# Value projections of four heads in one pass: 512 moving columns into four PSUM banks, with the gate projections moved between them

## The chip, the core and the metric

The kernel runs on one core of a Trainium2 chip, in one launch. Five engines work side by side, each with its own instruction stream: TensorE (PE, with its weight loads listed as PEld), VectorE (DVE), ScalarE (ACT), GpSimd (POOL) and SyncE (SP), which here issues nearly all DMA transfers. An engine runs its instructions in the order in which they stand; it waits on semaphores that other engines and transfers raise. The metric is the device time of one execution in microseconds (us), lower is better. The kernel before took 1098.91 us, the median of three runs (1098.56 to 1100.02).

## The reference, cut to what matters

One layer on 512 tokens of width 2048: a norm, one big projection `z = u @ w_in` (2048 by 8192), eight heads of chunkwise retention and eight heads of differential attention, gates, an output projection, and a gated side input.

```python
u = rmsnorm(h, attn_norm)
z = u @ w_in                       # rq 512 | rk 512 | rv 1024 | rg 1024 | dq 1024 | dk 1024 | dv 1024 | dg 1024 columns
rq, rk = rope(rq), rope(rk) * RET_DK ** -0.5
ro = retention(rq, rk, rv)         # chunks of 64: scores * decay inside, state across
ro = rmsnorm(ro) * ret_gn * silu(rg)
dq, dk = rmsnorm(dq), rmsnorm(dk)
attn = softmax(q0 k0) - lam * softmax(q1 k1)      # block-causal, per head
do = rmsnorm(attn @ dv) * diff_subln * 0.2 * silu(dg)
h = h + concat(ro, do) @ w_out
gate = sigmoid(rmsnorm(h) @ w_ple_gate)
out = h + gate * (p @ w_ple_proj)
```

Everything is float32. The two parts of a head that the change touches are `rv` and `dv`, the values: 128 columns of `w_in` for each head.

## The kernel before

**Precision.** A float32 operand is split into a high and a low part (`split`, lines 103 to 110: ACT writes the high part, DVE the difference). A product is three matmuls (`mm3`, lines 112 to 115): high by high, high by low, low by high, summed in PSUM. Line 113, 114 and 115 are these three, for every projection.

**Projections.** Tokens are the moving side for all but the values: `proj_fm` (line 170) makes the columns stationary, 128 at a time, and moves all 512 tokens, so that one call gives two blocks of 128 columns in two PSUM banks. The values are wanted with tokens on partitions: `proj_v` (line 180) makes 128 tokens stationary and moves 256 weight columns, the values of two heads; four token blocks share two banks, two blocks to a bank (`v_products`, line 140). A call of either kind runs over 16 blocks of the contraction, two at a time, and its weights come in four transfers of 512 KB through `wraw` (two buffers) and are split into `whi` and `wlo` (four buffers each). At the end `done(acc)` empties the banks: for the values `split_v` (line 193), which scales by the column `rcol` of the row norm.

**PSUM.** There are eight banks: four with the tag `acc` for projections, taken in turn; two `sc`, one `tp`, one `o` for everything else. A projection that takes a bank waits until what read that bank last is through.

**Order.** The program is written by hand and then scheduled. `run(job)` advances a projection; each `yield` is a tick of `clock`, and each tick also issues the steps that are due in `agenda`. The steps are the small work: norms of q and k (`QK`), scores and softmax (`SCORES`), transposes (`TURNS`), attention times values (`VALUES`) and the head's norm (`NORMS`), all at fixed numbers of ticks after a pair's `dk` is finished. The last norm of a pair comes 32 ticks after it. A projection is eight ticks long.

**Stages.** (1) `dv` of heads 0 and 1 together with `dq` of the same pair, while x and the weights still arrive (lines 276 to 304), then `row_norm` (line 208), which gives `rcol` and the row factor `R1`. This `dv0` takes two of the four `acc` banks. (2) The loop over four pairs of attention heads (line 476): dq, dk, dv, dg. (3) `rq0`, `rk0` into the four `acc` banks and `rv0` into the two `sc` banks (lines 489 to 492), with the steps of the last pair between them; then `flush`. (4) Retention, whose SBUF pools `rp` and `rc` take the memory of the attention pool `dp`: cosine and sine tables `cr` and `sr` are loaded (lines 504, 505) and multiplied by `R1`, `rope` (line 509) turns q and k, and rv1, rq1, rk1, rv2, rv3 follow, with retention steps `queue_ret` (line 562) after each value projection. (5) Gates, `w_out`, `w_gate`, outputs.

**Where a bank of q is read.** In `rope`, line 514 copies quarters of the bank (ACT), line 515 multiplies the bank by `cr` (DVE); only then is it free. So `rq0`'s banks are held until `cr` has been loaded.

Of the kernel before, what the change touches and what calls it, by code (L numbers as in the profile page):

```python
# [38 lines left out]
def f(ap):  # L39
    return ap.bitcast(F32)  # L40
# [3 lines left out]
def tile_layer(  # L44
# [86 lines left out]

    def fm_products(acc, k, nk, wh, wl, mh, ml):
# [137 lines left out]
    with ExitStack() as st:  # L270
        xp = st.enter_context(tc.tile_pool(name="xp", bufs=1))
        ssum = xp.tile([P, S], F32, name="ssum")

        warm = bank("tp", 1, "warm")
        wide = xp.tile([P, S], F32R, name="wide")
        nc.vector.memset(f(wide), 1.0)
        for _ in range(WARM):
            nc.tensor.matmul(warm, lhsT=wide[:, :P], rhs=wide, start=True, stop=True)  # L280
        start = [[bank(*tag, f"acc_{name}0_{j}") for j in range(2)]
                 for tag, name in ((("acc", 4), "dv"), (("sc", 2), "dq"))]
        for k in range(KB):
            xt = xp.tile([P, S], F32, tag=f"xt{k}", name=f"xt{k}")
            nc.sync.dma_start(xt, xT[k * P:(k + 1) * P, :])
            if k % 2 == 0:
                raw, wh, wl = ([wpool.tile([P, 2, CW], dt, tag=tag, name=f"{tag}{i}_{k}", bufs=n)
                                for i in range(2)] for tag, dt, n in
                               (("wraw", F32, 2), ("whi", F32R, 4), ("wlo", F32R, 4)))
            for i, off in enumerate((OFF_DV, OFF_DQ)):  # L290
                nc.sync.dma_start(raw[i][:, k % 2, :], w_in[k * P:(k + 1) * P, off:off + CW])
# [5 lines left out]
            for i in range(2):  # L297
                split(wh[i][:, k % 2, :], wl[i][:, k % 2, :], raw[i][:, k % 2, :])
# [51 lines left out]
    with ExitStack() as st:  # L350
# [29 lines left out]
        def diff_steps(h, pair):  # L380
# [118 lines left out]
    with ExitStack() as st:  # L499
# [62 lines left out]
        def queue_ret(h, qkv):  # L562
            s, v, n = ret_steps(h, qkv)
# [5 lines left out]
        for g in range(2):  # L569
            qkv = {}  # L570

            def q_done(acc, g=g, qkv=qkv):
                for j in range(2):
                    t = rope(acc[j], f"q{g}_{j}")
                    for i, (half, oth) in enumerate(((A0, A1), (A1, A0))):
                        qd = rc.tile([P, S], F32R, tag=f"qd{j}{i}", name=f"qd{g}_{j}{i}")
                        nc.scalar.activation(qd[half], t[half], AF.Copy)
                        nc.vector.tensor_copy(qd[oth], f(qd)[half])

                        qz = rc.tile([P, S], F32R, tag=f"qz{j}{i}", name=f"qz{g}_{j}{i}")  # L580
                        nc.gpsimd.memset(f(qz)[oth], 0.0)
                        nc.vector.tensor_tensor(qz[half], t[half], f(qd)[half], ALU.subtract)
                        qkv["q", 4 * g + 2 * j + i] = qd, qz

            def k_done(acc, g=g, qkv=qkv):
                for j in range(2):
                    t = rope(acc[j], f"k{g}_{j}")
                    for i, (half, oth) in enumerate(((A0, A1), (A1, A0))):
                        ks = rc.tile([P, S], F32R, tag=f"ks{j}{i}", name=f"ks{g}_{j}{i}")
                        nc.scalar.activation(ks[half], t[half], AF.Copy)  # L590
                        nc.vector.tensor_tensor(ks[oth], t[half], f(ks)[half], ALU.subtract)
                        qkv["k", 4 * g + 2 * j + i] = ks

            if g == 0:
                q_done(ahead[0])
                k_done(ahead[1])
            else:
                run(proj_fm(w_in, OFF_RQ + g * CW, KB, u_hi, u_lo, f"rq{g}", q_done))
                run(proj_fm(w_in, OFF_RK + g * CW, KB, u_hi, u_lo, f"rk{g}", k_done))
            for hp in range(2 * g, 2 * g + 2):  # L600
                def v_done(acc, hp=hp, qkv=qkv):
                    mine = {**qkv, "v": split_v(acc, rp, f"rv{hp}")}
                    queue_ret(2 * hp, mine)
                    queue_ret(2 * hp + 1, mine)

                if hp == 0:
                    v_done(ahead[2])
                else:
                    run(proj_v(OFF_RV + hp * CW, f"rv{hp}", v_done))
# [175 lines left out]
```

## Time and profile before

| what | us |
|---|---|
| three runs | 1098.91, 1098.56, 1100.02 |
| the profiled execution | 1099.53 |
| its span in the trace | 1097.8 |
| PE busy | 1085.7 |
| DVE busy | 652.9 |
| ACT busy | 569.4 |

The span is what the trace covers; about 1.7 us of the profiled execution lie outside it. Matmuls overlap one another in the trace: one starts before the one ahead has ended. So the time that a matmul costs is read from the distance of two starts, not from its duration; a PE that is busy for 99% of the span only says that no gap is longer than such an overlap. An engine's idle time is shown in square brackets behind an instruction, with what ended it; DMA issue is shown as SPq.

Columns of the views below. Timeline: start and duration in us, engine, line, operation, output<-inputs with their shapes, and how many like it follow one another (x). Busy time by stretch: the stretch in us, its length, then busy us (and instructions) of PE, PEld, DVE, ACT and POOL, the granted clock as a share of full speed, the DMA engines' busy share, and GB/s. Waits: who waits <- for whom, total us, how often, the longest. Groups: as in the timeline, then busy us in total, mean ns of one, idle us before them.

### The profile page before, as it was taken

The numbers are of one execution on the slowest core, as the hardware profiler recorded it, in microseconds if no ns is written. First come the engines' busy times: TensorE is split into PE (matmuls) and PEld (weight loads), VectorE is DVE, ScalarE is ACT, GpSimd is POOL, SyncE is SP. The second block draws the span as 40 slices with busy tenths as digits, with TensorE's granted clock in tenths as the row PEclk, the third lists the DMA queues.
The fourth block names the chain that finished last, engine by engine and source line by source line (L and its number), as shares of the span: only waits on it lengthen the run. The fifth ranks groups of instructions, "written<-read, shape, count | busy, mean of one in ns | idle before, by whom it ended". The sixth has DMA issues, their size and how long they took to land.

```text
span 1097.8 us, 14909 instructions
## 1 busy us (share of the span) xinstructions
PE 1085.7 (99%) x5668; PEld 930.9 (85%) x5668; DVE 652.9 (59%) x1210; ACT 569.4 (52%) x1049; POOL 4.9 (0%) x14
## 2 busy tenths in 40 slices
PE   9999999999999999999999999999999999999998
PEld 7988888888988988899879988888888888888887
DVE  7677679658765876485775576534433544333452
ACT  8477676657665756654674468333333343222330
POOL 0000000000000000000000000000000000000000
PEclk9999999999999999999999999999999999999999
DMA  7432321222222222233223223643333333443341
GB/s 238 132 97 77 96 78 59 91 82 77 78 92 81 78 77 84 90 116 102 84 84 96 90 87 94 211 136 97 100 99 99 97 93 105 123 127 106 125 134 39
DMA packets 104632, 111.22 MB, mean 101 GB/s; under 512 B 4464, under 2 KB 97008, under 8 KB 104560
## 3 DMA queue, kind: packets, MB, share of 16 engines
q1 hardware_dynamic: 101968, 105.55, 31.1%
q10 hardware_dynamic: 2592, 4.72, 1.3%
q8 instruction: 44, 0.72, 0.3%
q14 instruction: 28, 0.23, 0.1%
HBM read 106.06 MB, written 4.19 MB: 100 GB/s over the span
## 4 chain that ended last, share of the span: by engine, by line
PE 94%; DVE 3%; ACT 2%; issue 1%; DMA 0%; SPq 0%; ACTq 0%; DVEq 0%
PE acc_pg L113 5%; PE acc_pg L114 5%; PE acc_pg L115 5%; PE acc_o L115 5%; PE acc_o L113 5%; PE acc_o L114 5%; PE acc_rv L113 3%; PE acc_rv L115 3%; PE acc_rv L114 3%; PE acc_dg L113 3%; PE acc_rg L113 3%; PE acc_dg L114 3%; PE acc_dg L115 3%; PE acc_rg L115 3%; PE acc_rg L114 3%; PE acc_dq L113 3%
## 5 line engine op out<-in xcount | busy, mean ns | idle before, releaser
L106 ACT ACTIVATE wh_o<-wr_o 128x512 fp32r<-128x512 f32 x64 | 40.4, 631 | 115.8 <-PE acc_o L114 105.4
L113 PE MATMUL acc_o<-mh,wh_o 128*128 128x512 f32 x256 | 99.6, 389 | 0.0
L114 PE MATMUL acc_o<-ml,wh_o 128*128 128x512 f32 x256 | 99.6, 389 | 0.0
L115 PE MATMUL acc_o<-mh,wl_o 128*128 128x512 f32 x256 | 99.6, 389 | 0.0
L107 DVE TENSOR_TENSOR wl_o<-wr_o,wh_o 128x512 fp32r<-128x512 f32 x64 | 44.2, 691 | 92.8 <-ACT wh_o L106 92.8
L106 ACT ACTIVATE wh_pg<-wr_pg 128x512 fp32r<-128x512 f32 x56 | 35.3, 631 | 100.4 <-PE acc_pg L114 79.8
L114 PE MATMUL acc_pg<-hl,wh_pg 128*128 128x512 f32 x224 | 87.2, 389 | 0.0
L113 PE MATMUL acc_pg<-hh,wh_pg 128*128 128x512 f32 x224 | 87.2, 389 | 0.0
L115 PE MATMUL acc_pg<-hh,wl_pg 128*128 128x512 f32 x224 | 87.1, 389 | 0.0
L107 DVE TENSOR_TENSOR wl_pg<-wr_pg,wh_pg 128x512 fp32r<-128x512 f32 x56 | 38.6, 690 | 70.3 <-ACT wh_pg L106 70.3
L113 PE MATMUL acc_rv<-wh_rv,uh 128*128 128x256 f32 x256 | 72.5, 283 | 0.0
L115 PE MATMUL acc_rv<-wh_rv,ul 128*128 128x256 f32 x256 | 72.4, 283 | 0.0
L114 PE MATMUL acc_rv<-wl_rv,uh 128*128 128x256 f32 x256 | 72.4, 283 | 0.0
L114 PEld LDWEIGHTS acc_o<-ml,wh_o 128*128 128x128 f32 x256 | 48.1, 188 | 10.0
L115 PEld LDWEIGHTS acc_o<-mh,wl_o 128*128 128x128 f32 x256 | 48.1, 188 | 10.0
L113 PEld LDWEIGHTS acc_o<-mh,wh_o 128*128 128x128 f32 x256 | 48.1, 188 | 9.9
L113 PE MATMUL acc_dv<-wh_dv,uh 128*128 128x256 f32 x192 | 54.5, 284 | 0.0
L115 PE MATMUL acc_dv<-wh_dv,ul 128*128 128x256 f32 x192 | 54.3, 283 | 0.0
L114 PE MATMUL acc_dv<-wl_dv,uh 128*128 128x256 f32 x192 | 54.3, 283 | 0.0
L113 PE MATMUL acc_dg<-uh,wh_dg 128*128 128x512 f32 x128 | 51.3, 401 | 0.0
L113 PE MATMUL acc_dk<-uh,wh_dk 128*128 128x512 f32 x128 | 50.5, 394 | 0.0
L113 PE MATMUL acc_rg<-uh,wh_rg 128*128 128x512 f32 x128 | 50.2, 392 | 0.0
(313 smaller groups left out, 2968.2 us busy)
## 6 DMA issues: line engine op xcount, KB each, us to landing
wr_o<-w_out SPq DMA_DIRECT2D x32, 512.0 KB, 3.6
wr_pg<-w_gate SPq DMA_DIRECT2D x32, 512.0 KB, 3.6
wr_dk<-w_in SPq DMA_DIRECT2D x16, 512.0 KB, 3.6
wr_dg<-w_in SPq DMA_DIRECT2D x16, 512.0 KB, 3.5
wr_rv<-w_in SPq DMA_DIRECT2D x16, 512.0 KB, 3.6
wr_rg<-w_in SPq DMA_DIRECT2D x16, 512.0 KB, 3.7
wr_dq<-w_in SPq DMA_DIRECT2D x12, 512.0 KB, 3.6
wr_dv<-w_in SPq DMA_DIRECT2D x12, 512.0 KB, 3.6
```

The source lines that it names most:

```text
L106: nc.scalar.activation(hi, src, AF.Copy)
L107: nc.vector.tensor_tensor(lo, src, f(hi), ALU.subtract)
L113: nc.tensor.matmul(out, lhsT=ah, rhs=bh, start=start, stop=False, skip_group_check=True)
L114: nc.tensor.matmul(out, lhsT=ah, rhs=bl, start=False, stop=False, skip_group_check=True)
L115: nc.tensor.matmul(out, lhsT=al, rhs=bh, start=False, stop=stop, skip_group_check=True)
```

## The change

Values of four heads are projected in one pass. `wide_chunk` loads weights 512 columns wide, two blocks of the contraction per transfer of 512 KB; `wide_products` moves 512 columns against 128 stationary tokens, so each token block fills one bank, four blocks four banks; `proj_wide` runs it in 16 ticks. For the first and the last two blocks of the contraction it holds the work back and does token blocks 0 and 1 before 2 and 3, so that the first two banks are taken and given up earlier than the last two. Stage 1 now projects `dv` of heads 0 to 3, in all four `acc` banks. Heads 4 to 7 of `dv` follow in pair 2. `rv1` and `rv2` become one pass, before rq1; `rv0` and `rv3` stay as they are.

The gates move: dg0 and dg1 follow dk0, dg2 follows dk1, none follows the values, dg3 follows dk3.

```diff
+    def wide_products(acc, k, wh, wl, blocks):
+        for t in blocks:
+            c = slice(t * P, (t + 1) * P)
+            mm3(acc[t], u_hi[k][:, c], u_lo[k][:, c], wh, wl, k == 0, k == KB - 1)
...
+    def proj_wide(n0, name, done):
+        acc = [bank("acc", 4, f"acc_{name}_{t}") for t in range(4)]
+        held = []
+        for k, wh, wl in wide_chunk(n0, name):
+            if k in (0, 1, KB - 2, KB - 1):
+                held.append((k, wh, wl))
+                if k % 2:
+                    for blocks in ((0, 1), (2, 3)):
+                        for one in held:
+                            wide_products(acc, *one, blocks)
+                        if k == KB - 1:
+                            done(acc, blocks)
+                        if blocks[0] == 0:
+                            yield
+                    held = []
+                else:
+                    continue
+            else:
+                wide_products(acc, k, wh, wl, range(4))
+            yield
...
+    def split_wide(vs, acc, blocks):
+        n = S // len(vs)
+        for t in blocks:
+            for i, v in enumerate(vs):
+                split(v[0][:, t, :], v[1][:, t, :], acc[t][:, i * n:(i + 1) * n], rcol[:, t:t + 1])
...
-        start = [[bank(*tag, f"acc_{name}0_{j}") for j in range(2)]
-                 for tag, name in ((("acc", 4), "dv"), (("sc", 2), "dq"))]
+        start = [[bank(*tag, f"acc_{name}0_{j}") for j in range(n)]
+                 for n, tag, name in ((4, ("acc", 4), "dv"), (2, ("sc", 2), "dq"))]
...
-            v_products(start[0], k, wh[0][:, k % 2, :], wl[0][:, k % 2, :])
-            fm_products(start[1], k, KB, wh[1][:, k % 2, :], wl[1][:, k % 2, :], u_hi, u_lo)
+            split(vh, vl, vw)
+            split(qh, ql, qw)
+            wide_products(start[0], k, vh, vl, range(4))
+            fm_products(start[1], k, KB, qh, ql, u_hi, u_lo)
...
         for hp in range(4):
...
             run(proj_fm(w_in, OFF_DK + hp * CW, KB, u_hi, u_lo, f"dk{hp}", k_done))
-            if hp:
-                run(proj_v(OFF_DV + hp * CW, f"dv{hp}", v_done))
-            run(proj_fm(w_in, OFF_DG + hp * CW, KB, u_hi, u_lo, f"dg{hp}",
-                        lambda acc, hp=hp: silus(acc, [on_d[2 * hp + j] for j in range(2)], True)))
+            if hp == 2:
+                vals.append(values_of(dp, "dv1", S, 1))
+                run(proj_wide(OFF_DV + S, "dv1", partial(split_wide, vals[1:])))
+            for g in ((0, 1), (2,), (), (3,))[hp]:
+                gates(g)
...
+        q_done(0, ahead[0])
+        k_done(0, ahead[1])
+        v_done(0, ahead[2])
+        run(proj_wide(OFF_RV + CW, "rv1", wide_done))
+        run(proj_fm(w_in, OFF_RQ + CW, KB, u_hi, u_lo, "rq1", partial(q_done, 1)))
+        run(proj_fm(w_in, OFF_RK + CW, KB, u_hi, u_lo, "rk1", partial(k_done, 1)))
+        v_done(2)
+        run(proj_v(OFF_RV + 3 * CW, "rv3", partial(v_done, 3)))
```

How this moves instructions is shown at three places. In the names the first number behind `dk`, `rk` and the like is the pair, the next the bank, the last a running number; `[waits ...]` names the engine or queue whose semaphore the instruction waits for.

**PE at the end of stage 1**, where the row sums of the norm (`r1_ps`) are followed by dk0. Before:

```order
L226 MATMUL r1_ps_706<-s1l_694,ones_82 128x512
L113 MATMUL acc_dk0_0_791<-uh0_129,wh_dk0_0_795 128x512 [waits Activation_49]
L114 MATMUL acc_dk0_0_791<-ul0_130,wh_dk0_0_795 128x512
L115 MATMUL acc_dk0_0_791<-uh0_129,wl_dk0_0_796 128x512 [waits DVE_49]
L113 MATMUL acc_dk0_1_792<-uh0_129,wh_dk0_0_795 128x512
L114 MATMUL acc_dk0_1_792<-ul0_130,wh_dk0_0_795 128x512
L115 MATMUL acc_dk0_1_792<-uh0_129,wl_dk0_0_796 128x512
```

In the changed kernel (its line 277 is line 226 before):

```order
L277 MATMUL r1_ps_740<-s1l_728,ones_82 128x512
L113 MATMUL acc_dk0_0_825<-uh0_130,wh_dk0_0_829 128x512 [waits DVE_49]
L114 MATMUL acc_dk0_0_825<-ul0_131,wh_dk0_0_829 128x512
L115 MATMUL acc_dk0_0_825<-uh0_130,wl_dk0_0_830 128x512
L113 MATMUL acc_dk0_0_825<-uh1_166,wh_dk0_0_829 128x512
L114 MATMUL acc_dk0_0_825<-ul1_167,wh_dk0_0_829 128x512
L113 MATMUL acc_dk0_1_826<-uh0_130,wh_dk0_0_829 128x512 [waits DVE_49]
L114 MATMUL acc_dk0_1_826<-ul0_131,wh_dk0_0_829 128x512
```

Before, the first matmul of each dk0 bank waits for the split weights alone. Now each waits for DVE: dk0's two banks are the first two of dv0's four, and DVE reads them last.

**PE at the end of stage 3**, from the norm of the last attention head (`ss_d7`) to the next value projection (`acc_rv1`). Before:

```order
L259 MATMUL ss_d7_4804<-sqh_d7_4745,ones_82 128x512 [waits DVE_49,PE_49]
L113 MATMUL acc_rk0_0_4648<-uh14_631,wh_rk0_14_4815 128x512
L114 MATMUL acc_rk0_0_4648<-ul14_632,wh_rk0_14_4815 128x512
L115 MATMUL acc_rk0_0_4648<-uh14_631,wl_rk0_14_4816 128x512
...
L115 MATMUL acc_rk0_1_4649<-uh15_664,wl_rk0_14_4816 128x512
L113 MATMUL acc_rv0_0_4831<-wh_rv0_0_4835,uh0_129 128x256
L114 MATMUL acc_rv0_0_4831<-wl_rv0_0_4836,uh0_129 128x256
...
L115 MATMUL acc_rv0_1_4832<-wh_rv0_14_5037,ul15_665 128x256
L113 MATMUL acc_rv1_0_5171<-wh_rv1_0_5175,uh0_129 128x256 [waits Activation_49]
L114 MATMUL acc_rv1_0_5171<-wl_rv1_0_5176,uh0_129 128x256 [waits DVE_49]
```

Between ss_d7 and rv1 stand the last 12 matmuls of rk0 and all 192 of rv0. In the changed kernel:

```order
L310 MATMUL ss_d7_4614<-sqh_d7_4519,ones_82 128x512 [waits DVE_49,PE_49]
L113 MATMUL acc_rv0_0_4374<-wh_rv0_14_4625,uh14_660 128x256
...
L115 MATMUL acc_rv0_1_4375<-wh_rv0_14_4625,ul15_699 128x256
L113 MATMUL acc_rv1_0_4759<-wh_rv1_0_4765,uh0_130 128x512 [waits DVE_49]
...
L113 MATMUL acc_rv1_1_4760<-wh_rv1_0_4765,uh0_130 128x512 [waits DVE_49]
...
L115 MATMUL acc_rv1_1_4760<-wh_rv1_3_4835,ul3_243 128x512
L113 MATMUL acc_rv1_2_4761<-wh_rv1_0_4765,uh0_130 128x512 [waits DVE_49]
...
L113 MATMUL acc_rv1_3_4762<-wh_rv1_0_4765,uh0_130 128x512 [waits DVE_49]
...
L589 MATMUL rs0_0_4817<-qd0_00_4686,ks0_00_4728 128x512 [waits DVE_49,PE_49]
```

Between ss_d7 and rv1 there are now the last 24 matmuls of rv0 and nothing else. Behind them come 24 matmuls into banks 0 and 1 (three for each of four contraction blocks and two banks), nine into bank 2, nine into bank 3, and then the first scores (`rs0`). The first matmul into each of the four banks waits for DVE.

**DVE behind that norm**, from the end of head 7 (`ond7`) to the last of the four banks (`rt_k0_1`). Before:

```order
L435 SCALAR_TENSOR_TENSOR ond7_759<-ot7_4742,g_sub_96,ond7_759 128x512 [waits DVE_49]
L107 TENSOR_TENSOR wl_rv0_8_4952<-wr_rv0_8_4949,wh_rv0_8_4951 128x512 [waits DMAHW4_49,Activation_49]
L506 TENSOR_TENSOR cr_5083<-cr_5083,R1_99 128x512 [waits DMAHW6_49,DVE_49]
L107 TENSOR_TENSOR wl_rv0_10_4980<-wr_rv0_8_4949,wh_rv0_10_4979 128x512 [waits Activation_49]
L507 TENSOR_TENSOR sr_5084<-sr_5084,R1_99 128x512 [waits DMAHW7_49]
L515 TENSOR_TENSOR rt_q0_0_5090<-acc_rq0_0_4421,cr_5083 128x512 [waits DVE_49]
...
L515 TENSOR_TENSOR rt_k0_0_5132<-acc_rk0_0_4648,cr_5083 128x512 [waits DVE_49,Activation_49]
...
L515 TENSOR_TENSOR rt_k0_1_5147<-acc_rk0_1_4649,cr_5083 128x512 [waits Activation_49]
```

In the changed kernel:

```order
L486 SCALAR_TENSOR_TENSOR ond7_793<-ot7_4516,g_sub_96,ond7_793 128x512 [waits DVE_49]
L110 SCALAR_TENSOR_TENSOR vl_rv0_4750<-acc_rv0_0_4374,rcol_98,vh_rv0_4749 128x256 [waits Activation_49]
L110 SCALAR_TENSOR_TENSOR vl_rv0_4750<-acc_rv0_1_4375,rcol_98,vh_rv0_4749 128x256 [waits PE_49,Activation_49]
...
L561 TENSOR_TENSOR cr_4671<-cr_4671,R1_99 128x512 [waits DMAHW6_49]
L570 TENSOR_TENSOR rt_q0_0_4678<-acc_rq0_0_3907,cr_4671 128x512 [waits DVE_49]
L562 TENSOR_TENSOR sr_4672<-sr_4672,R1_99 128x512 [waits DMAHW7_49]
L570 TENSOR_TENSOR rt_q0_1_4699<-acc_rq0_1_3908,cr_4671 128x512
...
L572 TENSOR_TENSOR rt_q0_0_4678<-rt_q0_0_4678,zs_q0_0_4677 128x512 [waits DVE_49]
L572 TENSOR_TENSOR rt_q0_1_4699<-rt_q0_1_4699,zs_q0_1_4698 128x512 [waits DVE_49]
...
L570 TENSOR_TENSOR rt_k0_0_4720<-acc_rk0_0_4147,cr_4671 128x512 [waits DVE_49,Activation_49]
...
L570 TENSOR_TENSOR rt_k0_1_4735<-acc_rk0_1_4148,cr_4671 128x512 [waits Activation_49]
```

The sequence is the same work: the tables `cr` and `sr` after `ond7`, then q, then k. The splits of rv0 (`vl_rv0`) now stand ahead of the tables, and no weight split (`wl_...`) stands between q and k.

## Rows read from the trace of the kernel before

**Rows 1.** The page: busy time of TensorE, and its granted clock in 40 slices.

```profile
PE 1085.7 (99%) x5668; PEld 930.9 (85%) x5668; DVE 652.9 (59%) x1210; ACT 569.4 (52%) x1049; POOL 4.9 (0%) x14
PEclk9999999999999999999999999999999999999999
```

**Rows 2.** Busy time by stretch: rv0 alone (256 columns), then gates and w_out (512 columns).

```profile
468.00:492.00 24.00, 24.00 (x202) 24.00 (x201) 20.40 (x34) 13.34 (x23) 2.08 (x4) 1.00 0.42 130
700.00:796.00 96.00, 96.00 (x425) 79.54 (x424) 42.20 (x64) 33.46 (x56) 0.00 (x0) 1.00 0.36 115
```

**Rows 3.** The page's costliest groups: one of the three matmul lines of the retention values.

```profile
L113 PE MATMUL acc_rv<-wh_rv,uh 128*128 128x256 f32 x256 | 72.5, 283 | 0.0
```

**Rows 4.** Timeline of TensorE in stage 1, one contraction block, first instruction of each kind.

```profile
36.08 0.28 PE L113 MATMUL acc_dv<-whi,uh 128*128 128x256 f32 x1
...
37.51 0.40 PE L113 MATMUL acc_dq<-uh,whi 128*128 128x512 f32 x1
...
38.90 0.28 PE L113 MATMUL acc_dv<-whi,uh 128*128 128x256 f32 x1
```

**Rows 5.** Timeline of TensorE: the first matmuls of stage 1, and the first behind it.

```profile
5.76 0.63 PE L113 MATMUL acc_dv<-whi,uh 128*128 128x256 f32 x2
...
53.00 0.17 PE L220 MATMUL rc_ps<-ones,s1h 128*128 128x2 f32 x1
```

**Rows 6.** Timeline of three engines behind stage 1: TensorE's next, the value splits, dq's normalisation.

```profile
54.37 0.39 PE L113 MATMUL acc_dk<-uh,wh_dk 128*128 128x512 f32 x1
...
56.24 0.46 ACT L109 ACTIVATE vh_dv<-acc_dv,rcol 128x256 fp32r<-128x256 f32 x1
...
56.73 0.48 DVE L110 SCALAR_TENSOR_TENSOR vl_dv<-acc_dv,rcol,vh_dv 128x256 fp32r<-128x256 f32 x1 [0.99 <-ACT vh_dv L109]
...
61.48 1.28 DVE L450 TENSOR_TENSOR t_q<-acc_dq,R 128x512 f32<-128x512 f32 x2
```

**Rows 7.** Timeline of ScalarE: one copy of a whole bank.

```profile
444.77 0.60 ACT L430 ACTIVATE ot<-od 128x512 f32<-128x512 f32 x1
```

**Rows 8.** Timeline of TensorE: the norm of the last attention head.

```profile
464.81 0.40 PE L259 MATMUL ss_d<-sqh_d,ones 128*128 128x512 f32 x1
```

**Rows 9.** Timeline of VectorE behind it.

```profile
470.58 0.75 DVE L435 SCALAR_TENSOR_TENSOR ond<-ot,g_sub,ond 128x512 f32<-128x512 f32 x1
...
474.87 0.69 DVE L506 TENSOR_TENSOR cr<-cr,R 128x512 f32<-128x512 f32 x1 [2.66 <-DMA cr<-cosT]
...
476.68 0.69 DVE L515 TENSOR_TENSOR rt_q<-acc_rq,cr 128x512 f32<-128x512 f32 x1
...
479.08 0.69 DVE L517 TENSOR_TENSOR rt_q<-rt_q,zs_q 128x512 f32<-128x512 f32 x1
...
486.97 0.69 DVE L515 TENSOR_TENSOR rt_k<-acc_rk,cr 128x512 f32<-128x512 f32 x1
```

**Rows 10.** Waits of the DMA queue (total us, times, longest), and its issue of the cosine table.

```profile
SPq L504 <- DVE ond L435: 1.7, 1, 1.7
...
471.42 0.34 SPq L504 DMA_DIRECT2D cr<-cosT  x1
```

**Rows 11.** Timeline of ScalarE: halves of q, quarters of the banks of k.

```profile
479.86 1.29 ACT L577 ACTIVATE qd<-rt_q 64x512 fp32r<-64x512 f32 x2 [2.61 <-DVE rt_q L517]
...
484.86 3.01 ACT L514 ACTIVATE zs_k<-acc_rk 32x512 f32<-32x512 f32 x5
```

**Rows 12.** Busy time and granted clock by stretch at the end, behind the last matmul.

```profile
1093.50:1095.80 2.30, 0.00 (x0) 0.00 (x0) 1.08 (x3) 0.42 (x1) 0.00 (x0) 1.00 0.00 0
1095.90:1097.80 1.90, 0.00 (x0) 0.00 (x0) 0.00 (x0) 0.00 (x0) 0.00 (x0) 0.50 0.23 73
```

**Rows 13.** Waits of TensorE by line.

```profile
PE or L113 <- ACT onr L552: 1.6, 1, 1.6
PE ss_r L259 <- DVE sqh_r L252: 0.8, 1, 0.8
```

More of the change, by code (lines that the diff above doesn't have):

```diff
@@ L130, in wchunk, with wide_chunk @@
                 yield k0 + s, wh, wl
+    def wide_chunk(n0, name):
+        wv = w_in.rearrange("(kb p) n -> p kb n", p=P)
+        for k0 in range(0, KB, 2):
+            with tc.high_priority(offset=AHEAD):
+                raw = wpool.tile([P, 2, S], F32, tag="wraw", name=f"wr_{name}_{k0}", bufs=2)
+                nc.sync.dma_start(raw, wv[:, k0:k0 + 2, n0:n0 + S])
+            for k in range(2):
+                with tc.high_priority(offset=AHEAD):
+                    wh = wpool.tile([P, S], F32R, tag="whi", name=f"wh_{name}_{k0 + k}")
+                    wl = wpool.tile([P, S], F32R, tag="wlo", name=f"wl_{name}_{k0 + k}")
+                    split(wh, wl, raw[:, k, :])
+                yield k0 + k, wh, wl
     def fm_products(acc, k, nk, wh, wl, mh, ml):
@@ L285, in tile_layer @@
             nc.sync.dma_start(xt, xT[k * P:(k + 1) * P, :])
[L286 to L291, printed above, removed]
+            raw = wpool.tile([P, S + CW], F32, tag="wraw", name=f"wraw_{k}", bufs=2)
+            vw, qw = raw[:, :S], raw[:, S:]
+            nc.sync.dma_start(vw, w_in[k * P:(k + 1) * P, OFF_DV:OFF_DV + S])
+            nc.sync.dma_start(qw, w_in[k * P:(k + 1) * P, OFF_DQ:OFF_DQ + CW])
+            (vh, vl), (qh, ql) = ([wpool.tile([P, n], F32R, tag=t, name=f"{t}{n}_{k}", bufs=4)
+                                   for t in ("whi", "wlo")] for n in (S, CW))
             uh = upool.tile([P, S], F32R, tag=f"uh{k}", name=f"uh{k}")
@@ L472, in queue_heads, with gates @@
                     after(NORMS[j], n)
-            return v_done, qk_done("q", stack_q), qk_done("k", stack_k)
+            return qk_done("q", stack_q), qk_done("k", stack_k)
+        vals = [values_of(dp, "dv0", S, 1)]
+        def gates(hp):
+            run(proj_fm(w_in, OFF_DG + hp * CW, KB, u_hi, u_lo, f"dg{hp}",
+                        lambda acc: silus(acc, [on_d[2 * hp + j] for j in range(2)], True)))
         for hp in range(4):
-            v_done, q_done, k_done = pair_jobs(hp)
+            q_done, k_done = pair_jobs(hp)
             if hp == 0:
-                v_done(start[0])
+                split_wide(vals, start[0], range(4))
                 q_done(start[1])
@@ L567, in queue_ret @@
             due[0] += RET[5]
[L569 to L609, printed above, removed]
@@ new lines, in tile_layer, with q_done @@
+        qkv = {}
+        def q_done(g, acc):
+            for j in range(2):
+                t = rope(acc[j], f"q{g}_{j}")
+                for i, (half, oth) in enumerate(((A0, A1), (A1, A0))):
+                    qd = rc.tile([P, S], F32R, tag=f"qd{j}{i}", name=f"qd{g}_{j}{i}")
+                    nc.scalar.activation(qd[half], t[half], AF.Copy)
+                    nc.vector.tensor_copy(qd[oth], f(qd)[half])
+                    qz = rc.tile([P, S], F32R, tag=f"qz{j}{i}", name=f"qz{g}_{j}{i}")
+                    nc.gpsimd.memset(f(qz)[oth], 0.0)
+                    nc.vector.tensor_tensor(qz[half], t[half], f(qd)[half], ALU.subtract)
+                    qkv["q", 4 * g + 2 * j + i] = qd, qz
@@ new lines, in k_done, with v_done @@
+        def k_done(g, acc):
+            for j in range(2):
+                t = rope(acc[j], f"k{g}_{j}")
+                for i, (half, oth) in enumerate(((A0, A1), (A1, A0))):
+                    ks = rc.tile([P, S], F32R, tag=f"ks{j}{i}", name=f"ks{g}_{j}{i}")
+                    nc.scalar.activation(ks[half], t[half], AF.Copy)
+                    nc.vector.tensor_tensor(ks[oth], t[half], f(ks)[half], ALU.subtract)
+                    qkv["k", 4 * g + 2 * j + i] = ks
+        def v_done(hp, acc=None):
+            if acc:
+                qkv["v", hp] = values_of(rp, f"rv{hp}", CW, 2)
+                split_v(qkv["v", hp], acc)
+            queue_ret(2 * hp)
+            queue_ret(2 * hp + 1)
@@ new lines, in wide_done @@
+        def wide_done(acc, blocks):
+            for hp in (1, 2):
+                qkv.setdefault(("v", hp), values_of(rp, f"rv{hp}", CW, 2) if blocks[0] == 0 else None)
+            split_wide([qkv["v", 1], qkv["v", 2]], acc, blocks)
+            if blocks[0]:
+                v_done(1)
+        q_done(0, ahead[0])
[3 more added lines that the diff above has]
+        run(proj_fm(w_in, OFF_RQ + CW, KB, u_hi, u_lo, "rq1", partial(q_done, 1)))
```

25 lines of the change are left out of this document (10 added, 15 removed).

## Prediction

> **What bounds the kernel now.** First the page: TensorE is busy for 99% of the span, at full granted clock in all 40 slices [rows 1]. So every stage is bound by the rate at which matmuls start, and what counts is the cost of one and the places where TensorE would be made to wait. The stretches give the rate: 24.00 us of 256-column matmuls hold 201 or 202 starts, 119 to 120 ns each; 96 us of 512-column ones hold 424 or 425, 226 to 227 ns [rows 2]. A narrow matmul lasts 283 ns in the groups [rows 3], but that overlaps the next; the starts count. Then the timeline at the three places where the change touches waits: behind stage 1, around the norm of the last attention head, and the list of TensorE's waits for what the retention stalls on.
>
> **Wider matmuls: -6.8 us.** Six head-pair projections go wide (four of dv, rv1, rv2): each is 192 narrow matmuls (a line's 256 for four of them, [rows 3], is 64 for each, and there are three lines), 1152 in all, replaced by 576 wide. A pair saves 2 x 119.5 - 227 = 12 ns, by the ends of both rates 11 to 14; I take 13 for the 384 outside stage 1: 5.0 us. In stage 1 a narrow one took (37.51 - 36.08)/12 = 119 ns and a 512-column one (38.90 - 37.51)/6 = 232 ns [rows 4], a saving of only 7 ns; between that and 13 I take 9.5 by 192, 1.8 us. Bounds: 5.5 to 8.1.
>
> The Trainium skill (TensorE: Matmul & The Clock Gate, Back-to-back issue gap) puts the isolated distance of two matmuls at N/2.4 + 2.5 ns, so nearly all of it would go with the columns and a pair would save the 2.5 ns once. By that the 576 pairs would give an estimated 1.4 us and the sum would end near 1111.4; the spacings of 119.5 and 227 ns do not bear it out, and the measurement decides.
>
> **Stage 1: -1.2 us (0 to -1.6).** From the first matmul to the row sums it takes 53.00 - 5.76 = 47.2 us [rows 5], while 16 blocks at 2.82 us [rows 4] are 45.1: 2.1 us are lost to data that come late and to the clock at the start. With 12 wide and 6 dq matmuls a block takes about 12 x 0.227 + 1.39 = 4.1 us, while its transfers grow from 512 to 640 KB: 25% more data in 45% more time. So TensorE should wait less; I leave 0.9 us for the start, where the first, larger weights come later.
>
> **Behind stage 1: +3.3 us.** dv0 now holds all four `acc` banks, so dk0 starts only when DVE has read the first one. Count from Y = 53.00, the row sums. dk0 started at Y+1.4 with the split weights ready; the first `vh_dv` started at Y+3.2, since it needs `rcol` [rows 5, 6]. Its copy of a 512-column bank takes 0.60 us (a bank of `od` by ScalarE, [rows 7]), the low half on DVE some 0.7 (two 512-column products in 1.28, [rows 6], or 0.69 to 0.75, [rows 9]): the bank is free at Y+4.65, 3.3 later. The second bank comes 1.1 us behind, while TensorE still has work in the first. Bounds 2.6 (copies on a 256-column scale, 0.46 and 0.48, [rows 6]) to 4.5. What was hidden beneath the weights waiting in `whi` is now exposed, since nothing else is queued for TensorE there.
>
> **Clock behind that wait: +1.0 us (0 to 2.4).** At the end of the kernel the granted clock was still 1.00 in the 2.3 us behind the last matmul and 0.50 after that [rows 12]; over the 1.6 us wait in the retention it stayed at full [rows 1, 13]. TensorE will here do next to nothing for some 4.6 us, so a stretch at 1.2 GHz is likely; what it costs no row shows, and I take a value in the lower half.
>
> **End of stage 3: +12.0 us (9 to 14).** This is the term that decides. The tables `cr` and `sr` lie in memory of the attention pool: their load waited 1.7 us on the last `ond` and was issued 0.1 us behind it [rows 9, 10]. The q and k banks of head pair 0 are freed by products with `cr`, and rv1 wants these same four banks. Before, between the norm of head 7 (`ss_d`) and rv1 stood 12 matmuls of rk0 and 192 of rv0, 12 x 0.227 + 192 x 0.12 = 26 us of cover, and rv1 took two banks alone. Now dv3 no longer stands in that pair, the norm comes eight ticks later against the projections, and 24 narrow matmuls of rv0 (2.9 us) are left.
>
> Count from X, the start of `ss_d` (464.81, [rows 8]). In before `ond` ended at X+6.5, `cr` times R1 began at X+10.1 after 2.66 us of waiting for its transfer, the first product with q at X+11.9, its sum was done at X+15.0 and the first product with k began at X+22.2 [rows 9]. The dependencies are the same afterwards: `cr` at X+10.1 to 10.75, `rt_q0_0` to X+11.4 (bank 0 free), `sr` to 12.1, `rt_q0_1` to 12.8 (bank 1), the sum of q done at X+14.4 (0.6 earlier than before, no weight split between). Then ScalarE makes four halves `qd` at 0.645 (X+17.0) and four quarters of the first k bank at 0.60 [rows 11] (X+19.4), and DVE frees bank 2 at X+20.2. Four more quarters and a product: bank 3 at X+22.65. TensorE is through rv0 at X+0.3 + 2.9 = X+3.2. It waits 8.2 us for bank 0, has 24 matmuls in banks 0 and 1 (5.4 us, to X+16.9), waits 3.3 for bank 2, nine matmuls, then 0.4 for bank 3. That is 11.9, and 12.0 with the second bank. Bounds: 9 if ScalarE does k's quarters ahead of q's halves, 14 if the work behind the first wait runs at 1.2 GHz (below). SP's queue holds the next weights behind `cr`, but both weight buffers of rv1 can be filled during the wait.
>
> **Retention: -1.7 us (0 to -3.3), and other banks +0.5 (0 to 2).** TensorE waited 1.6 us in one place for `onr` before it could use the `o` bank, and 0.8 us for `sqh_r` [rows 13], together with their neighbours some 3.3, where rope of q1 occupies DVE and ScalarE. rv1 and rv2 are now both finished before rq1, so the heads of the second pair come a little sooner against that rope; I take half. Against it stand the other switches between four and two banks (dq3 behind dv1, rq1 behind rv1), each hidden by the two-step ending that frees banks 0 and 1 first, priced at 0.25 each; up to 1 each if not. Moving the gates changes which small steps fall beside which projection, not their number; I price it at nothing, +-1.5.
>
> **Sum:** -6.8 - 1.2 + 3.3 + 1.0 + 12.0 - 1.7 + 0.5 = +7.1 us. On the profiled execution's 1099.5 that is 1106.6; it lay 0.6 above the median of the three runs, so 1106.0.
>
> **Rivals.** (1) *Clock.* The waits behind stage 1 and in front of rv1 each leave TensorE at 1.2 GHz long enough to be felt: the first costs 2.4 instead of 1.0; in front of rv1 the 24 matmuls take 10.9 us instead of 5.4 and end at X+22.3, 2.1 past bank 2. Together +3.5: 1109.5. For it speaks the 0.50 behind the last matmul [rows 12]; against it that TensorE waits for bank 2 anyway, so that half speed there is mostly hidden. The Trainium skill (TensorE: Matmul & The Clock Gate, HAM oscillation) says that matmul bursts separated by waits pay for the fall and the return of the clock at every wait, which is a rule against this change; the trace agrees with the fall, at its end, and shows no return.
>
> (2) *The tables come early*, the faster one. If `cr` and `sr` got memory whose last reader is older than `ond7`, rope of q and k would be done beneath rv0, all four banks would be free at its end, and the 12.0 would be gone: 1094.0. The change pays as soon as this stall is under 12.0 - 7.1 = 4.9 us, and by over 2.2 us when it is under 2.7. For it: the products need only R1 and the inputs. Against it: the queue's wait is on `ond` itself [rows 10].
>
> (3) *No change:* the stall is halved, 5 to 7 us, because only one of the tables' halves waits and k's quarters overtake; then 1099 to 1101.
>
> **How the numbers follow.** Forecast 0.70, clock 0.16, early tables 0.06, no change 0.08. About 0.2% (2.2 us) is what a measurement of this kernel can tell from no change: 1096.7 to 1101.1. The forecast's own low end (wide saving 8.1, collisions -3.3, stall 9) reaches 1100.5, so a little of its chance lies there: faster 0.06, same 0.10, slower 0.84. The range from 1100.5 to 1111.0 holds the forecast and the clock rival and leaves out the early tables and most of (3).
>
> **What would show it.** Right: wide matmuls start every 0.227 us; TensorE waits about 3.3 us at the first `acc_dk0` for DVE's `vl_dv`; it waits about 8 us at `acc_rv` for the product of q and 2 to 3.5 for that of k; the clock row shows a dip in both slices; the wait for `onr` shrinks. Wrong: no gap between rv0 and rv1 (early tables), a saving per pair near zero, or new waits of TensorE in the attention loop, which I priced at nothing.

## The result, and the profile after

The changed kernel takes 1112.67 us (median of four runs, 1111.61 to 1113.81), the kernel before 1098.98 (four runs): a ratio of 1.0123, 95% interval 1.0106 to 1.0141. The forecast was 1106.0, its range 1100.5 to 1111.0. The direction was right; 13.7 us are lost where 7.1 were forecast, and the time lies outside the range. The profiled execution took 1113.35 us with a span of 1111.2, 13.4 more than before.

The page after, busy time and granted clock, beside [rows 1]:

```profile
PE 1086.1 (98%) x5092; PEld 905.3 (81%) x5092; DVE 651.6 (59%) x1194; ACT 568.1 (51%) x1033; POOL 4.9 (0%) x14
PEclk9989999999999999998999999999999999999999
```

576 instructions fewer on TensorE, and the clock is no longer full in two slices: those of 56 to 83 and of 500 to 528 us. The list of TensorE's waits after (who <- for whom, total us, times, longest) names what stands there, beside [rows 13]:

```profile
PE acc_rv L113 <- DVE rt_q L570: 9.3, 1, 9.3
PE acc_dk L113 <- DVE vl_dv L110: 3.2, 1, 3.2
PE or L114 <- DVE sl L107: 2.3, 2, 1.7
PE acc_rv L113 <- DVE rt_k L570: 0.7, 1, 0.7
PE or L113 <- ACT onr L607: 0.3, 1, 0.3
```

The waits in front of dk0 and of rv1 that the prediction named are there and are the longest; neither was in the list before. The one for the product of k, forecast at 2 to 3.5 us, is 0.7. In place of the wait for `onr`, 0.3 now, there is one of 1.7 for `sl`. What they leave behind is seen in the busy time by stretch after (columns as in [rows 2]; the clock is the third number from the end):

```profile
9.00:60.00 51.00, 51.00 (x226) 42.24 (x225) 35.13 (x73) 28.83 (x55) 0.00 (x0) 1.00 0.56 170
76.80:83.30 6.50, 6.08 (x14) 4.80 (x15) 3.96 (x7) 2.98 (x6) 0.00 (x0) 0.50 0.06 20
83.30:90.00 6.70, 6.70 (x31) 5.52 (x30) 3.63 (x6) 3.03 (x5) 0.00 (x0) 1.00 0.27 79
500.90:506.50 5.60, 5.54 (x13) 4.30 (x14) 5.43 (x11) 2.48 (x4) 0.00 (x0) 0.50 0.00 0
594.90:598.50 3.60, 3.60 (x12) 2.81 (x11) 3.53 (x8) 2.65 (x5) 0.00 (x0) 0.55 0.36 126
```

In stage 1 a matmul of 512 columns starts every 226 ns, as it should (51.00 / 226). Behind the wait at dk0, behind the one at rv1 and behind a third in the retention the clock is at 1.2 GHz: 14 starts in 6.5 us, 31 in the 6.7 us that follow. TensorE at dk0, from the first row sum over the wait to the first matmul at full speed:

```profile
72.49 0.17 PE L271 MATMUL rc_ps<-ones,s1h 128*128 128x2 f32 x1
...
77.22 0.80 PE L113 MATMUL acc_dk<-uh,wh_dk 128*128 128x512 f32 x1 [3.21 <-DVE vl_dv L110]
...
83.33 0.40 PE L115 MATMUL acc_dk<-uh,wl_dk 128*128 128x512 f32 x1
```

dk0 starts 4.73 us behind the row sums. Its first 14 matmuls take 6.11 us, where 14 x 227 ns are 3.18. VectorE in front of rv1, beside [rows 9]:

```profile
494.43 0.75 DVE L486 SCALAR_TENSOR_TENSOR ond<-ot,g_sub,ond 128x512 f32<-128x512 f32 x1
...
499.49 0.69 DVE L561 TENSOR_TENSOR cr<-cr,R 128x512 f32<-128x512 f32 x1 [1.80 <-DMA cr<-cosT]
500.22 0.69 DVE L570 TENSOR_TENSOR rt_q<-acc_rq,cr 128x512 f32<-128x512 f32 x1
...
509.25 0.69 DVE L570 TENSOR_TENSOR rt_k<-acc_rk,cr 128x512 f32<-128x512 f32 x1
```

The norm of head 7 on TensorE, and the issue of the cosine table:

```profile
488.42 0.39 PE L310 MATMUL ss_d<-sqh_d,ones 128*128 128x512 f32 x1
```

```profile
495.29 0.34 SPq L559 DMA_DIRECT2D cr<-cosT  x1
```

With X = 488.42, `cr` came at X+11.1 and the first product at X+11.8, where the prediction had X+10.1 and X+10.75.

Where the 13.4 us came from can be counted. Each matmul's distance to the next start, less 227 ns for 512 columns or 120 for 256 (and so on), is time lost there; what is left is the count of matmuls. How much is lost in a stretch hangs on the price put on the smallest matmuls; the differences do not:

| stretch | lost before | lost after | difference | forecast |
|---|---|---|---|---|
| count and width of matmuls | | | -7.5 | -6.8 |
| to the row sums | 4.2 | 3.2 | -1.0 | -1.2 |
| row sums, dk0, attention loop | 8.6 | 15.0 | +6.4 | +3.3 +1.0 |
| rq0, rk0, rv0, to the first scores | 0.4 | 14.0 | +13.6 | +12.0 |
| rest of retention, gates, outputs | 4.7 | 6.6 | +1.9 | -1.7 |
| sum | | | +13.4 | +7.1 with 0.5 for other banks |

### The profile page after: what moved, and what is told of

Its sections match the earlier page's. It is cut to its first block, busy times and chain, and to the rows that moved or that the text cites. A ratio compares the mean times of both kernels' runs of the same rounds, so it can differ in the third digit from the quotient of the medians.

```text
span 1111.2 us, 13720 instructions
## 1 busy us (share of the span) xinstructions
PE 1086.1 (98%) x5092; PEld 905.3 (81%) x5092; DVE 651.6 (59%) x1194; ACT 568.1 (51%) x1033; POOL 4.9 (0%) x14
## 4 chain that ended last, share of the span: by engine, by line
PE 91%; ACT 4%; DVE 3%; DMA 1%; issue 1%; SPq 0%; ACTq 0%
PE acc_pg L114 5%; PE acc_pg L115 5%; PE acc_pg L113 5%; PE acc_o L115 5%; PE acc_o L113 5%; PE acc_o L114 5%; PE acc_dg L113 3%; PE acc_dq L113 3%; PE acc_dq L115 3%; PE acc_dq L114 3%; PE acc_dg L114 3%; PE acc_dg L115 3%; PE acc_rg L113 3%; PE acc_rg L114 3%; PE acc_rg L115 3%; PE acc_dv L113 2%
## 5 line engine op out<-in xcount | busy, mean ns | idle before, releaser
L113 PE MATMUL acc_rv<-wh_rv,uh 128*128 128x256 f32 (+1 forms) x192 | 62.9, 328 | 10.0 <-DVE rt_q L570 9.3
L115 PE MATMUL acc_rv<-wh_rv,ul 128*128 128x256 f32 (+1 forms) x192 | 62.1, 324 | 0.0
L114 PE MATMUL acc_rv<-wl_rv,uh 128*128 128x256 f32 (+1 forms) x192 | 62.1, 323 | 0.0
L114 PE MATMUL acc_dk<-ul,wh_dk 128*128 128x512 f32 x128 | 51.0, 399 | 0.0
L115 PE MATMUL acc_dk<-uh,wl_dk 128*128 128x512 f32 x128 | 50.7, 398 | 0.0
L115 PE MATMUL acc_rg<-uh,wl_rg 128*128 128x512 f32 x128 | 49.9, 390 | 0.0
```

Source lines behind the costliest of these rows:

```text
L113: nc.tensor.matmul(out, lhsT=ah, rhs=bh, start=start, stop=False, skip_group_check=True)
L114: nc.tensor.matmul(out, lhsT=ah, rhs=bl, start=False, stop=False, skip_group_check=True)
L115: nc.tensor.matmul(out, lhsT=al, rhs=bh, start=False, stop=stop, skip_group_check=True)
```

## The experiments

All are edits of the changed kernel (1112.7), timed against the kernel before on the same chip (1099.2 to 1099.8 in these runs).

**e1: two narrow matmuls for each wide one.**

```diff
-            mm3(acc[t], u_hi[k][:, c], u_lo[k][:, c], wh, wl, k == 0, k == KB - 1)
+            for i in range(2):
+                w = slice(i * CW, (i + 1) * CW)
+                mm3(acc[t][:, w], u_hi[k][:, c], u_lo[k][:, c], wh[:, w], wl[:, w],
+                    k == 0 and i == 0, k == KB - 1)
```

> The changed kernel (1112.7), but each 512-column value matmul is two of 256 columns into the two halves of the same bank; order, banks, transfers and waits stay. Theory (start spacing of 119.5 and 227 ns): 576 pairs by 12 to 13 ns, so +7 us, 1119.5 to 1120.5. Rival (the isolated-gap rule, 2.5 ns a pair): +1.4 us, 1114.1. Second rival (the value matmuls are not what changed, all gain came from stage 1's data): within 1 us of 1112.7.

Measured 1117.19: +4.5, between the theories. The busy time of stage 1 in e1, in the same 51 us as above:

```profile
9.00:60.00 51.00, 51.00 (x363) 47.94 (x362) 34.96 (x72) 28.32 (x54) 0.00 (x0) 1.00 0.55 166
```

A block has 30 matmuls here and 18 there: 51.00 x 30/363 = 4.215 us against 51.00 x 18/226 = 4.062, and 0.153 by the 12 pairs of a block is 13 ns a pair. So the price by starts is 13 ns, and the rival of 2.5 ns a pair is out. But the whole moved by only 4.5: by the two rates the 576 pairs cost 7.5 us more, and 3.3 us less are lost elsewhere (1.2 at rv1, where TensorE arrives later at the same wait, 0.8 in the attention loop and at dk0, 0.8 at the start, 0.5 in the retention). e7 takes this up.

**e2: dk0 in banks of its own.** dq0 goes to the `tp` and `o` banks, the row sums to `sc`:

```diff
-        pc = bank("tp", 1, "rc_ps")
+        pc = bank("sc", 2, "rc_ps")
...
-        pr = bank("o", 1, "r1_ps")
+        pr = bank("sc", 2, "r1_ps")
...
+                 [bank(("tp", "o")[j], 1, f"acc_dq0_{j}") for j in range(2)]]
...
+                         ("acc", 4) if hp else ("sc", 2)))
```

> The changed kernel, but dq of heads 0 and 1 is summed in the tp and o banks, the row sums in the two sc banks, and dk0 then runs in the sc banks, so that it does not wait for the values' copies. Theory (the wait for vl_dv costs 3.4 us and the 16 matmuls at 1.2 GHz behind it 3.3): both go, 1106.0. Rival (the pause of the row norm alone lowers the clock, so the slow matmuls stay): -3.4, 1109.3. Rival (the wait only moves to the split weights or to t_q): 1112.

Measured 1104.99: -7.7, the theory and a little more (in this profile 0.9 less is lost ahead of the row sums, 0.6 less in front of the first scores and 0.7 less in the retention, where the clock did not fall). TensorE in e2 at dk0; the row sums began at 71.57:

```profile
72.93 0.41 PE L113 MATMUL acc_dk<-uh,wh_dk 128*128 128x512 f32 x1
73.17 0.39 PE L114 MATMUL acc_dk<-ul,wh_dk 128*128 128x512 f32 x1
```

dk0 starts 1.36 us behind them, as before the change, and at full speed (0.24 us from one start to the next). So the short pause of the row norm does not lower the clock; the wait for the banks does.

**e3: the tables early.** Their memory is that of the last scores of head 7:

```diff
...
+        def load_tables():
+            for src, name in ((cosT, "cr"), (sinT, "sr")):
+                t = tab.tile([P, S], F32, tag="p1", name=name)
+                nc.sync.dma_start(t, src)
+                tabs.append(t)
...
+            if hp == 3:
+                after(22, load_tables)
+                after(25, scale_tables)
```

> The changed kernel, but the cosine and sine tables lie in tiles that the last scores of head 7 give up, and are loaded and multiplied by R1 beneath rv0; rope of k still comes behind q's halves, whose memory waits for ond7. Theory (rv1's stall is the tables' memory): the 9.4 us wait for q's banks goes; a wait of 3 to 4 us for k's banks is left, with up to 2.6 us of slow clock: 1104 (1102 to 1106). Rival (the stall is the end of head 7's norm whatever the tables do): 9 us are left, 1111 to 1113.

Measured 1104.22, as expected. By the count of losses 6.0 of the 8.5 us between the two profiles lie in this stretch; 1.1 lie ahead of the row sums and 1.1 in the retention, where the clock did not fall. TensorE's wait in e3:

```profile
PE acc_rv L113 <- DVE rt_k L581: 4.7, 1, 4.7
```

The 9.3 us for q's product are gone, the stall for k's has grown from 0.7 to 4.7: with q out of the way it is the next in line.

**e4: idle matmuls where TensorE would wait.**

```diff
+    def spin(n, name):
+        b = bank("tp", 1, f"spin_{name}")
+        for _ in range(n):
+            nc.tensor.matmul(b, lhsT=u_hi[0][:, :P], rhs=u_hi[0], start=True, stop=True)
...
         row_norm(ssum)
+        spin(13, "a")
...
+        spin(40, "b")
         q_done(0, ahead[0])
```

> The changed kernel with idle matmuls of 512 columns into the free tp bank where TensorE would wait: 13 in front of dk0, 40 in front of rv1. They compute nothing that is used. Theory (the slow clock costs 3.3 us at dk0, but at rv1 it is hidden under the wait for k's banks): -3, 1109.7; the trace then shows full clock at both places and a wait of about 3.5 us for rt_k. Rival (the slow matmuls cost their time at both places): -5.6, 1107. Rival (the clock falls in spite of the matmuls, or they delay dk0): 1112 to 1114.

Measured 1108.37: -4.3. Clock and waits in e4 (the stretch behind the row sums, the one in front of rv1; then the waits):

```profile
75.00:83.00 8.00, 7.74 (x34) 6.03 (x33) 6.39 (x10) 5.58 (x10) 0.00 (x0) 1.00 0.17 57
493.50:502.00 8.50, 8.30 (x37) 6.47 (x36) 7.01 (x13) 2.16 (x4) 0.39 (x1) 1.00 0.30 111
```

```profile
PE acc_rv L113 <- DVE rt_k L576: 2.8, 1, 2.8
PE ss_r L315 <- DVE sqh_r L308: 0.7, 1, 0.7
PE acc_dk L113 <- DVE vl_dv L110: 0.3, 1, 0.3
PE acc_rv L113 <- DVE rt_q L576: 0.2, 1, 0.2
```

The clock stays full at both places. By the count of losses dk0 and the attention loop give 2.7 us back, rv1 only 0.5: there the wait for k's product grows from 0.7 to 2.8, which is what the slow matmuls had covered. The spans of the two profiles differ by 4.9; the rest is 0.7 in the retention, where the clock did not fall, and 1.0 at the start, where executions differ by as much. So the clock was a real cost at dk0 and almost none at rv1, as the theory had it.

**e5: e3, with q and k rotated beneath rv0 as well.**

```diff
...
+                for j in range(2):
+                    after(26 + j, lambda j=j: turned.append(rope(ahead[0][j], f"q0_{j}")))
+                for j in range(2):
+                    after(29 + j, lambda j=j: turned.append(rope(ahead[1][j], f"k0_{j}", tab, "p0")))
```

> The changed kernel with the tables loaded early and the rotation of q and k of pair 0 done beneath rv0 as well, so that all four banks are free when rv1 begins. Theory (the whole stall in front of rv1 is these banks): TensorE goes from rv0 to rv1 without a wait; of the 13.3 us that were lost there 0 to 2 are left (the first scores may wait for q's halves): 1099.4 to 1101.4. Rival (the stall moves to head 0's scores or to the split weights, since ScalarE and VectorE get this work at once): 1104 or more, with the early tables alone.

Measured 1101.27 (eleven runs), in the range of the theory. The profiled execution is the slowest of them (1103.38); in it 3.2 us are still lost in this stretch, more than the 0 to 2 expected. TensorE goes from rv0 to rv1 without a wait, and meets the next one at the first scores, whose `sc` banks still hold rv0:

```profile
PE acc_dk L113 <- DVE vl_dv L110: 3.2, 1, 3.2
PE rs L603 <- DVE vl_rv L110: 2.4, 1, 2.4
```

**e6: e5 and e2 together.** No further edit.

> e5 and e2 together: dk0 in its own banks and the rotation beneath rv0. Theory (the two places are independent and the rest of the change is worth 7 to 8 us less the retention's 1 to 2): 1092 to 1094, faster than the kernel before by 0.5%. Rival (each removal lets the other stall grow): 1096 or more.

Measured 1095.96 (ratio to before 0.9964, 0.9952 to 0.9977): 0.4% faster than the kernel before, but 2 us short of the expectation and at the edge of the rival. That rival is not what happened: neither of the two stalls is left in its profile. What it has is the 2.3 us wait for rv0's split and slow matmuls behind it (below).

**e7: e6 with narrow pairs**, edited as e1.

> e6 with two matmuls of 256 columns in place of each of 512, as in e1. Here nothing else waits for the values, so the pair's price stands alone. Theory (13 ns a pair): 7.5 us above e6. Rival (8 ns a pair, which e1's 4.5 us would give): 4.5 us above e6.

Measured 1101.11, 5.2 above e6. In both kernels the executions differ in their mean granted clock, and their times with it. At 0.999 to 1.000 e7 took 1100.6 to 1101.2, e6 and e9 (below, the same at this place) 1093.7 to 1093.9; at 0.998 e7 took 1102.8 to 1103.1, e6 1095.2 to 1096.5. Like with like, the difference is about 7 us both times, a little under the theory's 7.5; the median of e6 is one of the executions at 0.998, that of e7 is not. So I read the pair at 12 to 13 ns, and e1's smaller sum as waits that close up when TensorE is later.

**e8: heads 2 and 3 one tick later.**

```diff
             if blocks[0]:
+                due[0] = clock[0] + RET[6] + 1
                 v_done(1)
```

> The changed kernel with the steps of heads 2 and 3 one tick later against rq1, as they stood in the kernel before. Theory now (the stalls beside rope of q1 are about as large at either tick, since rope holds VectorE and ScalarE for the same time): within 0.7 of 1112.7. Rival (the prediction's: one tick sooner is worth 1.7): 1114.4. Rival (the tick sooner is what costs, 1.9 with the slow clock behind it): 1110.8.

Measured 1111.85, 0.8 less: just outside what was expected of no effect. The traces say where it lies: the first scores of the retention, ahead of all that this edit moves, start at 512.80 in e8's profile and at 514.32 in the changed kernel's. So the 0.8 us are no effect of the tick. The waits of e8 show what a tick does:

```profile
PE or L113 <- ACT onr L607: 1.9, 2, 1.6
PE ss_r L310 <- DVE sqh_r L303: 0.8, 1, 0.8
```

These are the two of [rows 13], come back: the tick decides which step stands behind the rope of q1, not whether one does. What it is worth can be read from the time of rq1 and rk1, from the first matmul of rq1 to the first of rv3, in all kernels that hold the same 234 matmuls there:

| tick | clock in this stretch | profiles | us |
|---|---|---|---|
| sooner | falls behind the 1.7 us wait | changed kernel, e1, e5, e11 | 54.1 to 54.2 |
| sooner | full | e2, e3, e4, e6, e7, e9 | 53.4 to 53.5 |
| later | full | e8, e12 | 54.3 |

The busy time of 3.6 us at the same place behind the 1.7 us wait, first in e2, then in e11:

```profile
587.20:590.80 3.60, 3.60 (x18) 2.97 (x18) 3.53 (x7) 3.34 (x6) 0.00 (x0) 1.00 0.39 131
```

```profile
575.30:578.90 3.60, 3.60 (x12) 2.89 (x11) 3.53 (x8) 2.65 (x5) 0.00 (x0) 0.60 0.35 119
```

So the sooner tick is worth 0.8 us where the clock stays full, and the fall takes 0.7 of it back.

**e9: heads 0 and 1 one tick later, on e6.** The line of e8, put in front of `v_done(0, ahead[2])`.

> e6 with the steps of heads 0 and 1 of the retention one tick later, so that the first scores no longer wait 2.3 us for rv0's split in the two sc banks. Theory: that wait and the six slow matmuls behind it (1.6 us) go, 1092 to 1093. Rival (the wait goes to head 0's values or to the second pair's steps): 1095 to 1096.

Measured 1096.25, no gain. The first scores did not move against rv1 in the instruction order, so this tested nothing of the wait. It is useful for another reason: e6 and e9 have the same wait there, and their profiles differ behind it. First e6, then e9 (TensorE's first scores, then the 4 us behind):

```profile
501.74 0.47 PE L604 MATMUL rs<-qd,ks 128*128 128x512 f32 x1 [2.34 <-DVE vl_rv L110]
...
502.00:506.00 4.00, 4.00 (x14) 3.24 (x14) 3.25 (x6) 1.04 (x2) 0.00 (x0) 0.59 0.31 111
```

```profile
500.95 0.47 PE L604 MATMUL rs<-qd,ks 128*128 128x512 f32 x1 [2.36 <-DVE vl_rv L110]
...
502.00:506.00 4.00, 4.00 (x22) 3.43 (x21) 3.24 (x7) 1.68 (x3) 0.15 (x1) 1.00 0.17 62
```

The same 2.3 us of waiting, once with a fall of the clock and once without. The five executions of e9 took 1093.65 and 1093.83 at a mean granted clock of 1.000, and 1096.25, 1096.35 and 1096.35 at 0.998; the profiled one is the fastest. By the count of losses 1.6 of the 2.4 us between the two profiles lie behind this wait; the other 0.8 lie ahead of the row sums, where the clock is the same, so that not all of the 2.5 us between the executions is shown to be the clock's.

**e10: head 3 four ticks later, on e9.**

```diff
             queue_ret(2 * hp)
+            if hp == 1:
+                due[0] += 4
             queue_ret(2 * hp + 1)
```

> e9 with head 3 four ticks later as well, so that its scores come behind rope of q1 instead of beside it. Theory (the 1.9 us wait for sl and the 0.8 us wait for sqh_r of rk1 are rope's products ahead of them on VectorE and ScalarE): about 2.5 us less than e9, 1090. Rival (the same stalls come beside rope of k1): as e9 or slower.

Measured 1096.53: no gain. The 1.7 us for `sl` is down to 0.5, and 1.5 us stands at head 3's scores instead:

```profile
PE rs L604 <- DVE sf L609: 1.5, 1, 1.5
PE or L114 <- DVE sl L107: 0.5, 1, 0.5
```

**e11: rv0 split first, on e6.**

```diff
+        qkv["v", 0] = values_of(rp, "rv0", CW, 2)
+        split_v(qkv["v", 0], ahead[2])
         q_done(0, ahead[0])
         k_done(0, ahead[1])
-        v_done(0, ahead[2])
+        v_done(0)
```

> e6 with the split of rv0 written ahead of q's and k's halves, so that the two sc banks are free when the first scores want them. Theory (that wait is the split's place in the queue of VectorE): the 2.3 us wait goes, and with it the slow matmuls that follow it in some executions: 1092 to 1094. Rival (the halves come 1.9 us later instead and the scores wait for them): 1095 to 1096.5.

Measured 1093.77 (1093.60 to 1094.11; ratio to before 0.9947, 0.9933 to 0.9961): the fastest version of all. The 2.3 us have become 1.1 us for the halves of k, and the five executions lie within 0.5 us:

```profile
PE rs L604 <- DVE ks L660: 1.1, 1, 1.1
```

**e12: e8's tick on e11.**

> e11 with the steps of heads 2 and 3 one tick later, as in e8. If e8's 0.8 us was the tick: 0.8 less than e11. If it was chance: within 0.7 of e11.

Measured 1094.31, 0.5 above e11, within 0.7 as expected of chance. In e11's profile the clock fell behind the 1.7 us wait, in e12's, which does not have this wait, it did not; rq1 and rk1 take 54.2 and 54.3 us (table at e8).

## Why the prediction was wrong

The waits at dk0 and at rv1 came where and for the reason that was forecast. Three steps failed, all to the same side: the gain in the retention, which did not come, and the sizes of the slow clock behind dk0's wait and of the stall at rv1.

- *Wider matmuls, -6.8:* -7.5 by the starts, confirmed by e1's stage 1 and by e7. Right; in stage 1, too, a pair saves 13 ns, not 9.5.
- *Stage 1, -1.2:* -1.0 in this profile, up to 1.2 more in those of the experiments. Right within what executions differ by.
- *Behind stage 1, +3.3:* 3.4 (start of the row sums to dk0: 4.7 us, 1.36 before). e2 takes the wait away and the time goes with it. Right, though the terms given add up to 3.1 and not 3.3.
- *Clock behind that wait, +1.0:* this step failed in size. 14 matmuls at 1.2 GHz took 6.1 us in place of 3.2: 2.9 us, above even the bound of 2.4 (2.0 in e3's profile, 2.5 in e1's). I had no row for what a slow stretch costs behind a wait, and took a value in the lower half of a range that was itself too short and had no working. The Trainium skill's rule (TensorE: Matmul & The Clock Gate, HAM oscillation) that a burst behind a wait pays for the clock was weighed as a rival at 0.16; e2 and e4 bear it out at dk0, and e4 shows that at rv1 it costs next to nothing.
- *End of stage 3, +12.0:* 13.6, inside its bounds of 9 to 14. The chain was the forecast one (tables behind `ond7`, q, then k), as e3 and e5 show by taking it apart. It began about 1.0 us later: `cr` was multiplied 4.2 us behind its issue, not 3.45, and `ond7` ended 0.2 later. That the slow clock is hidden there by the wait for bank 2 held: the slow matmuls filled that wait, so 0.7 us of it show in place of 2 to 3.5, and 2.8 in e4, where the clock stays full.
- *Retention, -1.7:* this step failed in its mechanism, and it is the largest miss: +1.9. The prediction took a shorter wait for `onr` to be time gained. That wait did shrink, and one of 1.7 us for `sl` took its place, since VectorE and ScalarE are taken by the rope of q1 whichever step stands behind it (e8 and e10 move the steps, and other waits come). Over rq1 and rk1 the losses fell by 0.1 us in place of 1.7. The sooner tick is worth 0.8 with the clock at full (table at e8), but here the clock fell behind the 1.7 us wait (594.90 above): by its starts 1.4 us, of which the vanished 0.8 us wait for `sqh_r` covers half. The rest of the +1.9 was not in the sum at all: 1.1 beneath rv1, of which 0.7 stand at head 0's values, right behind the late rope of k0, and 0.9 beneath the gates, of which 0.4 stand at head 6; what causes the rest of these two is not shown.
- *Other banks, moved gates:* in e2 the row norm and the attention loop lose 0.2 us more than before. As priced, or a little under.

Of the rivals the early tables were not what the kernel does, but e5 bears out the price put on them: 11.4 us gone, where 12.0 were forecast. Yet the time is then 1101.3 and not 1094.0, so that the change does not pay with this stall at 3.2 us, where the prediction had it pay under 4.9; only without the wait at dk0 too does it gain. The clock rival came nearest with 1109.5, for half the right reason: its 2.4 at dk0 was near, its 2.1 at rv1 was hidden. The range left out that these terms could miss together: two of them, the clock and the retention, hang on the same thing, pauses of TensorE whose sequel I had not priced. Its low end was also added up wrongly: by the three terms named it is 1100.1, not 1100.5.

The prediction also said that no row shows what slow matmuls cost and that the trace before shows no return of the clock. Its first microseconds have a hint of both: matmuls of 256 columns start 0.21 us apart there and 0.12 from 7 us on, though the granted clock of the profile's rows is 1.00 on both sides:

```profile
6.40 0.41 PE L115 MATMUL acc_dv<-whi,ul 128*128 128x256 f32 x1
6.62 0.41 PE L113 MATMUL acc_dv<-whi,uh 128*128 128x256 f32 x1
...
7.39 0.28 PE L113 MATMUL acc_dv<-whi,uh 128*128 128x256 f32 x1
7.51 0.28 PE L114 MATMUL acc_dv<-wlo,uh 128*128 128x256 f32 x1
```

So what one slow matmul costs could have been estimated from these starts; how many of them follow a wait could not.

## What to carry to other kernels

A pair of matmuls made one saves 13 ns, which is little beside the banks that it takes: before a projection is given all the banks of a tag, follow each bank to its last reader, and that reader to the memory and the transfers it waits for. A wait of TensorE should be priced at its length plus the slow matmuls behind it, unless another wait follows at once and covers these. When one cause of a stall is removed, look at once for the next in line (q's bank, then k's, then the split of rv0). Here the wide order paid only with the stalls at dk0 and at rv1 both gone (e6, 0.4%); the split of rv0 put first made it 0.5% (e11). And when a step is moved so that a wait shrinks, look for the wait that takes its place before a gain is counted.

## What the hardware showed that I had not expected

The fall of the clock is not decided by the length of the wait alone. A wait of 1.7 us in the retention was followed by a clock of 0.55 in the profile of the changed kernel and by full clock in those of e2, e3, e4, e6, e7 and e9; at the first scores the same 2.3 us went either way in e6 and e9, and the executions of such a kernel lie 2 to 2.5 us apart with it. Those of e11, with 1.1 us there, lie within 0.5 us, though its profile shows the slow clock behind the 1.7 us wait. Why it went one way or the other stays open. Nor is the price of a fall the sum of its slow starts: behind the 1.7 us wait these cost 1.4 us, the stretch of rq1 and rk1 became only 0.7 longer, because a later wait was then gone. Idle matmuls kept the clock at full over 3 and 9 us of waiting (e4), which gained 2.7 us where nothing else covered the slow matmuls.
